# Three edits to the small products of a two-layer trunk: quarters of the array, one stretch of scores, and ends of heads one by one

## The chip, the cores and the metric

The kernel runs on one core of a Trainium2 chip. The metric is the device time in microseconds (us) of one launch, as the median of several runs; lower is better. The core has five engines that each work through their own list of instructions in order: TensorE (PE, matrix products), VectorE (DVE), ScalarE (ACT), GpSimd (POOL) and SyncE (SP), whose queue issues the transfers from memory. Products land in PSUM, in banks of 128 rows by 512 words; everything else lies in SBUF. Both have 128 rows (partitions).

## What is computed

Two layers work on 512 tokens of width 1024, in float32. Layer 0 mixes tokens with two groups of heads over one input projection: four mLSTM heads (64-wide keys, 128-wide values) and four gated DeltaNet heads (128 wide). Layer 1 mixes with eight HGRN2 heads. After each mixer, and after each gated feed-forward part, comes a normalised residual addition.

```python
for layer in range(DEPTH):
    u = rms_norm(x, norm_gains[layer, 0])
    mix = ab_mixer(u, ...) if layer % 2 == 0 else hgrn2_mixer(u, ...)
    x = x + rms_norm(mix, norm_gains[layer, 1])
    u = rms_norm(x, norm_gains[layer, 2])
    x = x + rms_norm(conv_ffn(u, ...), norm_gains[layer, 3])
```

Per chunk of tokens, an mLSTM head does the following; `num / den` is then normalised per head and multiplied by a sigmoid gate:

```python
s = jnp.einsum("bhld,bhsd->bhls", q_, k_) * d
num = jnp.einsum("bhls,bhsv->bhlv", s, v_) + w_inter[..., None] * jnp.einsum("bhld,bhdv->bhlv", q_, C)
den = jnp.sum(s, -1) + w_inter * jnp.einsum("bhld,bhd->bhl", q_, n)
C = carry_decay[..., None, None] * C + jnp.einsum("bhl,bhld,bhlv->bhdv", wk, k_, v_)
```

A DeltaNet head solves a unit lower triangular system per chunk and then scans over the chunks:

```python
sol = lax.linalg.triangular_solve(a_mat, rhs, left_side=True, lower=True, unit_diagonal=True)
v_new = u_ - jnp.einsum("bhld,bhdv->bhlv", w_, state)
o = jnp.einsum("bhld,bhdv->bhlv", qd_, state) + jnp.einsum("bhls,bhsv->bhlv", attn_, v_new)
state = gl_[..., None, None] * state + jnp.einsum("bhld,bhlv->bhdv", kd_, v_new)
```

An HGRN2 head has the same kind of scan, with the state decayed per key dimension. Each head's output is normalised by the root of its mean square and gated.

## The kernel before

The projections run with channels on the partitions and all 512 tokens along the row. Weights arrive by DMA as `raw`; ACT makes a rounded copy `whi` of them, DVE or POOL the remainder `wlo`, and each product of 128x512 is done three times (`whi` with `uh`, `whi` with `ul`, `wlo` with `uh`), 24 of them for one block of 128 channels. In the profile these are `pf` (input projections and feed-forward), `pt` (projections with tokens on the partitions) and `mo` at L127 (output projection). They are called full products here. The heads' own products are small: float32, 128x128 or less. A float32 product leaves two records in the profile, a full product one.

The order of each engine's list is fixed when the kernel is built. A planner walks through the program, puts each instruction where its cost table says it is ready, and fills the wait of a small product with full products of work that is due later. `tc.issue_after(x)` holds back what is issued under it until `x` has its place; `in_a_row` (L1102) uses this to keep a list of products behind its first one. Heads are generators: `run_head` starts one up to its `yield`, and `end_heads` runs the rest of it later, after the next head's projections have been written.

Layer 0 works two heads at a time in the order gdn(0), mlstm(0), gdn(1), mlstm(1).

- `gdn_pair` (L1108) inverts the triangular matrices, 128x128 for each of 4 chunks and 2 heads. Each is built from quarters of 64x64. `doubled` (L1205, with the products at L1210 and L1212) grows the inverse of the diagonal quarters level by level; at last `pp` (L1226) and `pd` (L1230) make the lower left quarter, eight products of 64x64 each: `pp` takes the rows `lo` and puts all eight in the rows `hi`, `pd` goes the other way, with ACT's copy of `pp` between them (L1227). Then each head scans its four chunks (`vn` L1245 and L1247, `S` L1252, `o` L1253 and L1255) and ends: squares on ACT (`chunk_squares`, L754), the root `rsqrt` on DVE (an integer guess and three Newton steps, eleven instructions with the one that makes its argument), then `head_out`: `yn`, four transposes on PE into `yt`, the gate, and the split into `yhi` (ACT) and `ylo` (DVE).
- `mlstm_pair` (L1274) makes 16 score products `ms` (L1298; 64x64 tiles, 128 columns: 4 chunks, 2 heads, 2 halves of the keys), multiplies them by the decays `dec` on DVE, makes 6 state additions `C` (L1305), adds the states up on DVE (`mC`), and then the outputs: 8 products `mo`<-`vaug` (L1320) and 6 `mo`<-`mC` (L1326). The end of both heads follows together: eight squares, one root over 128x8, then `head_out` twice.

Layer 1's mixer `c_mix` works in pairs too; `pair` makes the scores by levels (`lev` from `qf`, `kr`, and at last `mid`), assembles `at`, and for each head transposes the keys (`kdt`), copies them (`kt`), and scans. The last pair is j = 3.

The output projection of each layer needs `yhi` and `ylo` of all eight heads; the products that need the last head come last. Before layer 0's output projection stands mlstm(1), before layer 1's the pair j = 3.

In the token norms, the root uses ACT's Sqrt from a table (`tk_y`), which takes an `ACT_TABLE_LOAD` when another table was in use.

Of the kernel before, what the change touches and what calls it, by code (L numbers as in the profile page):

```python
# [18 lines left out]
P = 128  # L19
S = 512  # L20
D = 1024
NT = S // P
# [12 lines left out]
def kernel(  # L35
# [734 lines left out]
    def gate_block(wcols, u, new, func, eng=None):  # L770

        gs = new("gs")
        A.activation(out=gs, in_=feature_block(wcols, u, eng), func=func)
        return gs


    def ab_mix(pm, u, x0, g0):
# [274 lines left out]
        def decay_t(row, cvec, sub):  # L1052

            ps = mxt("rowbc")
            T.matmul(ps, lhsT=picks[:, row : row + 1].broadcast_to([P, P]), rhs=rows, start=True, stop=True)
            d = s("dec")
            tt(V, v4(d), v4(ps), bc(cvec, P), ALU.subtract if sub else ALU.add)
            G.affine_select(  # L1058
                out=v4(d), in_=v4(d), pattern=[[0, NT], [1, P]], compare_op=ALU.is_ge, fill=-BIG, base=0,
                channel_multiplier=-1,  # L1060
            )
            A.activation(out=d, in_=d, func=AF.Exp)
            return d, ps
# [44 lines left out]
        def gdn_pair(j, k, q, vf, gates):  # L1108
# [108 lines left out]
            for a in range(2):  # L1217
                tt(V, xx[lo, a * NT : (a + 1) * NT], pzs[a][lo, 0], bm(identc[lo], NT), ALU.add)
            for rs in (hi, lo):
                for a in range(2):  # L1220
                    tt(V, v4(mts[a])[rs, :, rs], pzs[a][rs, 1], bm(identc[rs], NT), ALU.add)
            if j == 0:
                fill(32, e)
            pp = chunks(mxt("pp"))
            for c in range(PC):
                T.matmul(pp[hi, c], lhsT=mc[c][lo, hi], rhs=xx[lo, c], start=True, stop=True)  # L1226
            A.copy(out=xx[hi], in_=pp[hi])  # L1227
            pd = chunks(mxt("pd"))
            for c in range(PC):
                T.matmul(pd[lo, c], lhsT=xx[hi, c], rhs=mc[c][hi, hi], start=True, stop=True)  # L1230
            for a in range(2):
                A.copy(out=v4(mts[a])[lo, :, hi], in_=pd[lo, a * NT : (a + 1) * NT])
# [41 lines left out]
        def mlstm_pair(j, k, q, gss):  # L1274
# [9 lines left out]
            ds = [decay_t(2 * j + a, c1[:, :, 2 * j + a], False)[0] for a in range(2)]  # L1284
            pt = mxt("mkt")
# [8 lines left out]
            for c, cs in enumerate(css):  # L1294
                for a, hs in enumerate(heads):
                    for ps in heads:
                        ks = slice(c * P + ps.start, c * P + ps.stop)
                        T.matmul(mss[a][ps, cs], lhsT=k[hs, ks], rhs=q[hs, cs], start=True, stop=True)  # L1298
            for a in range(2):
                tt(V, ds[a], mss[a], ds[a], ALU.mult)  # L1300

            pc = bank("sc", "C")[:, : 3 * (P + 1)].rearrange("p (c n) -> p c n", c=3)
            for c in range(NT - 1):
                for a, hs in enumerate(heads):
                    T.matmul(pc[hs, c], lhsT=v4(kw)[:, c, hs], rhs=vaug[2 * j + a][:, c, :], start=True, stop=True)  # L1305
# [32 lines left out]
            for a in range(2):  # L1338
                chunk_squares(ss[:, 4 * a : 4 * a + 4], hm[:, a])
# [4 lines left out]
            stt(v, ss, 0.5 / P, v, ALU.mult, ALU.add)  # L1344
            r = rsqrt(v, 8, "ml")
            for a in range(2):
                i = 2 * j + a
                ylo[i] = eighth(i, "ylo", F32R)
                head_out(
                    yhi[:, i, :], ylo[i], hm[:, a], r[:, 4 * a : 4 * a + 4], gss[a], bank("sc", "yt"),  # L1350
                    cmix[:, 88 + i : 89 + i],
                )
# [38 lines left out]
    def c_mix(pm, u, first, lb, olb, olbq, cnorm, maskc):  # L1391
# [25 lines left out]
        def pair(j, states, gates):  # L1417
# [104 lines left out]
            gss, pos = gates(), []  # L1522
            for a, (_, _, qk, _) in enumerate(states):
                h = 2 * j + a
                qb, kb, at = qk[:, 0, :], qk[:, 1, :], ats[a]
                for hf in (slice(0, 64), slice(64, P)):
                    A.copy(out=v4(at)[hf, :, hf], in_=atcs[a][hf])
                for i in range(2):
                    A.copy(out=v4(at)[:64, i::2, 64:], in_=pm_[i * 64 : (i + 1) * 64, a])
                tot = tots[a]  # L1530
                pt = bank("sc", "kdt")
                transpose4(pt, kb, range(NT))
                kt = s("kt")
                A.copy(out=kt, in_=pt)
                st = None
# [16 lines left out]
                pos.append(po)  # L1552
            yield
            ss = col(8, "mss")
            for a, po in enumerate(pos):
                chunk_squares(ss[:, 4 * a : 4 * a + 4], v4(po))
            r = mean_rsqrt(ss, 8, P, "ml")
            for a, po in enumerate(pos):
                h = 2 * j + a
                ylo[h] = eighth(h, "ylo", F32R)  # L1560
                head_out(yhi[:, h, :], ylo[h], v4(po), r[:, 4 * a : 4 * a + 4], gss[a], bank("sc", "yt"))
# [32 lines left out]

        def gate(h):
            ps = feature_block(cols_of(3072, h), u, V)
            gs = s("gs")
            A.activation(out=gs, in_=ps, func=AF.Sigmoid)
# [166 lines left out]
```

## Time and profile before

| | |
|---|---|
| median of 3 runs | 1320.03 us (1319.99 to 1321.26) |
| profiled execution | 1320.03 us, span 1318.3 us |
| mean granted TensorE clock | 0.999 |
| PE busy | 1302.2 us, 99% of the span |
| DVE, ACT, POOL busy | 662.6, 603.8, 368.5 us |
| layer 0's mixer | about 10 to 275 us |
| layer 0's feed-forward part | about 275 to 720 us |
| layer 1's mixer | about 720 to 925 us |
| layer 1's feed-forward part | about 925 us to the end |

A row of the timeline reads: start in us, duration in us, engine, line of the kernel, operation, output<-inputs by their names in the program, tile size on PE, shape, xN for N records in one row. Brackets at the end give the idle time of the engine just before, and what ended it. Durations on PE contain the time in its pipeline, so rows overlap; what a product costs PE is read from the start of one row to the start of the next. A row of the windows gives the stretch, its length, then the busy time and number of records of PE, weight loads (PEld), DVE, ACT and POOL, the granted PE clock, the DMA share and GB/s. A row of the waits gives the total in us, how often, and the longest. A row on a tile (`tk_y`) gives the smallest, median and largest duration in ns, and the first and last start.

### The profile page before, as it was taken

The page shows a single profiled execution, that of the slowest core. Times are in us where ns is not written, and L with a number is a line of the kernel's source. Part 1 is how long each engine was busy: PE and PEld are TensorE (multiplying, and loading weights), DVE is VectorE, ACT ScalarE, POOL GpSimd, SP SyncE. Part 2 cuts the span into 40 slices and gives each one's busy share as a digit, 9 for nine tenths or more (in the row PEclk, how much of TensorE's full clock was granted, in tenths as well). Part 3 has the DMA queues.
Part 4 walks back from the last instruction along what each step waited for, and adds up shares of the span by engine and source line. Part 5 has one row for each costly group of instructions (what it writes and reads, how often), then busy time and mean ns, then how long its engine had stood idle before and what let it go on. Part 6 is the DMA issues. An engine that isn't in the chain of part 4 may idle for free.

```text
span 1318.3 us, 19346 instructions
## 1 busy us (share of the span) xinstructions
PE 1302.2 (99%) x7581; PEld 1084.3 (82%) x7581; DVE 662.6 (50%) x1310; ACT 603.8 (46%) x1164; POOL 368.5 (28%) x200
## 2 busy tenths in 40 slices
PE   8999999999999999999999999999999999999998
PEld 8878888879888888888888888887888888888886
DVE  6875684567533333311376784976764333331114
ACT  6764563455433333322456654655554333333222
POOL 1000010002655555544200000000065555554440
PEclk9999999999999999999999999999999999999999
DMA  7521221243333333222305123231243333322211
GB/s 201 144 65 40 63 74 39 81 144 112 113 97 99 99 99 102 94 99 96 112 7 154 65 65 93 83 97 30 84 128 96 96 96 97 99 101 93 98 56 64
DMA packets 164697, 121.18 MB, mean 92 GB/s; under 512 B 8382, under 2 KB 150142, under 8 KB 164606
## 3 DMA queue, kind: packets, MB, share of 16 engines
q1 hardware_dynamic: 164606, 119.94, 29.9%
q8 instruction: 60, 0.98, 0.3%
q14 instruction: 31, 0.25, 0.1%
HBM read 117.83 MB, written 2.10 MB: 91 GB/s over the span
## 4 chain that ended last, share of the span: by engine, by line
PE 90%; ACT 4%; DVE 3%; DMA 1%; issue 1%; POOL 0%; SPq 0%; DVEq 0%; ACTq 0%; POOLq 0%
PE pf L127 49%; PE dn L127 15%; PE mo L124 4%; PE dn L124 3%; PE pf L124 3%; PE pt L127 2%; PE pt L124 2%; PE mo L127 2%; PE lev L1474 1%; PE ut L124 1%; ACT junk L754 1%; DMA raw<-in_ab_w_in_dram 1%; DVE wlo L99 1%; ACT whi L228 1%; DMA raw<-in_c_w_in_dram 1%
## 5 line engine op out<-in xcount | busy, mean ns | idle before, releaser
L99 POOL TENSOR_TENSOR wlo<-raw,whi 128x1024 fp32r<-128x1024 f32 x122 | 294.5, 2415 | 594.7 <-ACT whi L228 587.1
L127 PE MATMUL pf<-ul,whi 128*128 128x512 f32 x1040 | 408.1, 392 | 0.0
L127 PE MATMUL pf<-uh,whi 128*128 128x512 f32 x1040 | 407.2, 392 | 0.0
L127 PE MATMUL pf<-uh,wlo 128*128 128x512 f32 x1040 | 406.5, 391 | 0.0
L228 ACT CAST whi<-raw 128x1024 fp32r<-128x1024 f32 x192 | 201.0, 1051 | 222.0 <-PE pf L127 208.5
L102 DVE SCALAR_TENSOR_TENSOR acc<-pf,fcw,acc 128x511 f32<-128x511 f32 (+1 forms) x176 | 131.8, 749 | 274.2 <-ACT acc L306 271.1
L127 PEld LDWEIGHTS pf<-ul,whi 128*128 128x128 f32 x1040 | 195.3, 188 | 40.0
L127 PEld LDWEIGHTS pf<-uh,whi 128*128 128x128 f32 x1040 | 195.3, 188 | 39.8 <-issue 0.2
L127 PEld LDWEIGHTS pf<-uh,wlo 128*128 128x128 f32 x1040 | 195.3, 188 | 39.5
L99 DVE TENSOR_TENSOR hl<-h,hh 128x512 fp32r<-128x512 f32 x44 | 32.0, 727 | 161.7 <-ACT hh L589 161.7
L127 PE MATMUL dn<-whi,hh 128*128 128x512 f32 x288 | 112.2, 390 | 0.0
L127 PE MATMUL dn<-whi,hl 128*128 128x512 f32 x288 | 112.1, 389 | 0.0
L127 PE MATMUL dn<-wlo,hh 128*128 128x512 f32 x288 | 112.1, 389 | 0.0
L99 DVE TENSOR_TENSOR wlo<-raw,whi 128x1024 fp32r<-128x1024 f32 x70 | 85.1, 1221 | 41.9 <-ACT whi L228 41.5
L589 ACT CAST hh<-h 128x512 fp32r<-128x512 f32 x44 | 27.4, 623 | 155.2 <-PE dn L127 131.5
L1058 POOL TENSOR_SCALAR_AFFINE_SELECT dec<-dec 128x512 f32<-128x512 f32 x8 | 8.4, 1049 | 222.8 <-DVE dec L99 175.6
L306 ACT ACTIVATE acc<-pf,fcb,fcw 128x512 f32<-128x512 f32 x88 | 68.2, 775 | 4.2 <-PE pf L124 3.2
L99 POOL TENSOR_TENSOR sg<-sg,acc 128x512 f32<-128x512 f32 x44 | 57.8, 1313 | 25.5 <-ACT sg L565 25.5
L127 PEld LDWEIGHTS dn<-whi,hh 128*128 128x128 f32 x288 | 54.1, 188 | 11.6 <-issue 0.5
L127 PEld LDWEIGHTS dn<-wlo,hh 128*128 128x128 f32 x288 | 54.1, 188 | 11.3
L127 PEld LDWEIGHTS dn<-whi,hl 128*128 128x128 f32 x288 | 54.1, 188 | 11.2
L565 ACT ACTIVATE sg<-acc 128x512 f32<-128x512 f32 x44 | 27.8, 632 | 68.2 <-DVE acc L102 68.2
(383 smaller groups left out, 1816.3 us busy)
## 6 DMA issues: line engine op xcount, KB each, us to landing
raw<-in_ffn_w_up_dram SPq DMA_DIRECT2D x88, 512.0 KB, 3.7
raw<-in_ffn_w_down_dram SPq DMA_DIRECT2D x44, 512.0 KB, 3.3
raw<-in_c_w_in_dram SPq DMA_DIRECT2D x32, 512.0 KB, 4.3
raw<-in_ab_w_in_dram SPq DMA_DIRECT2D x26, 512.0 KB, 3.6
gain<-in_norm_gains_dram SPq DMA_DIRECT2D x8, 512.0 KB, 3.7
raw<-in_ab_w_out_dram SPq DMA_DIRECT2D x8, 512.0 KB, 3.7
raw<-in_c_w_out_dram SPq DMA_DIRECT2D x8, 512.0 KB
x<-in_x_dram SPq DMA_DIRECT2D x4, 512.0 KB
```

The source lines that it names most:

```text
L99: return eng.tensor_tensor(out=o, in0=a, in1=b, op=op)
L102: return V.scalar_tensor_tensor(out=o, in0=a, scalar=s, in1=b, op0=op0, op1=op1, **kw)
L124: last[eng] = f(**kw)
L127: f(**kw)
L228: A.copy(out=hv, in_=rv)
L306: A.activation(out=acc, in_=ps, func=AF.Identity, scale=taps[:, K - 1 : K], bias=bias)
L565: A.activation(out=sg, in_=ag, func=AF.Sigmoid)
L589: A.copy(out=hi, in_=hT[k])
L754: A.activation(out=junk[:, :P], in_=src[:, c, :], func=AF.Square, accum_out=ss[:, c : c + 1])
L1058: G.affine_select(out=v4(d), in_=v4(d), pattern=[[0, NT], [1, P]], compare_op=ALU.is_ge, fill=-BIG, base=0, channel_multiplier=-1,)
L1474: e = T.matmul(pls[a][i * 64 : (i + 1) * 64, c], lhsT=krs[a][:, c * P + i * 64 : c * P + (i + 1) * 64], rhs=qfs[a][:, :, at : at + 32], st ...
```

## The change

1. The inverse's last products. `pp` alternates between head 1 and head 0, and head 1's results go to the rows `lo` instead of `hi`; the second head's factors get a tile `x1` of their own (tag `sig`, one more DVE addition). `pd` alternates too, into two PSUM banks, with rows `lo` for head 1 and `hi` for head 0. ACT copies `pp` in two halves. Both sequences are kept by `in_a_row`.
2. The mLSTM's scores and additions. One `in_a_row` holds the addition of chunk 0 and head 1, then all 16 scores (by chunk, then half of the keys, then head), then the other five additions. Before, the scores' order was chunk, head, half. The two multiplications by the decays follow the stretch.
3. The last two heads of a layer. mLSTM pair 1 and the pair j = 3 of layer 1 end one head after the other: four squares, a root over 128x4 and `head_out` for the first, then for the second. The root is `table_rsqrt`: Sqrt on ACT, then a reciprocal, two multiplications and one combined step on DVE. `load_roots` does a Sqrt of ones ahead of it, behind the last gate and, in layer 0, the last decay. For j = 3, both heads' key transposes and copies come first (the second copy in tag `f`), then both scans, then the ends.

```diff
+    def table_rsqrt(v, n, st):
+        y, q = col(n, st + "_y"), col(n, st + "_q")
+        A.activation(out=y, in_=v, func=AF.Sqrt, scale=2.0)
+        V.reciprocal(out=y, in_=y)
+        tt(V, q, y, y, ALU.mult)
+        tt(V, q, q, v, ALU.mult)
+        r = col(n, st + "_y")
+        stt(r, q, 1.5, y, ALU.subtract, ALU.mult, reverse0=True)
+        return r
+
+    def load_roots(*after):
+        one = col(1, "tk_y")
+        V.memset(one, 1.0)
+        with ExitStack() as st:
+            for e in after:
+                st.enter_context(tc.issue_after(e.ins))
+            A.activation(out=one, in_=one, func=AF.Sqrt)
...
+            x1 = chunks(s("sig"))
+            tt(V, x1[lo, :NT], pzs[1][hi, 1], bm(identc[hi], NT), ALU.add)
+            pp = chunks(mxt("pp"))
+
+            def first(c, a):
+                ac = a * NT + c
+                return T.matmul(pp[(hi, lo)[a], ac], lhsT=mc[ac][lo, hi], rhs=xx[lo, ac], start=True, stop=True)
+
+            in_a_row(first, [(c, a) for c in range(NT) for a in (1, 0)])
...
-            pp = chunks(mxt("pp"))
-            for c in range(PC):
-                T.matmul(pp[hi, c], lhsT=mc[c][lo, hi], rhs=xx[lo, c], start=True, stop=True)
-            A.copy(out=xx[hi], in_=pp[hi])
-            pd = chunks(mxt("pd"))
-            for c in range(PC):
-                T.matmul(pd[lo, c], lhsT=xx[hi, c], rhs=mc[c][hi, hi], start=True, stop=True)
+            A.copy(out=xx[hi, :NT], in_=pp[hi, :NT])
+            A.copy(out=x1[lo, NT:], in_=pp[lo, NT:])
+            pds = [chunks(mxt("pd")) for _ in range(2)]
+
+            def second(c, a):
+                lhs, rhs = (x1[lo, NT + c], x1[lo, c]) if a else (xx[hi, c], mc[c][hi, hi])
+                return T.matmul(pds[a][lo, c], lhsT=lhs, rhs=rhs, start=True, stop=True)
+
+            in_a_row(second, [(c, a) for c in range(NT) for a in (1, 0)])
...
+            if j:
+
+                load_roots(last["gate"], last["decay"])
...
-            for c, cs in enumerate(css):
-                for a, hs in enumerate(heads):
-                    for ps in heads:
-                        ks = slice(c * P + ps.start, c * P + ps.stop)
-                        T.matmul(mss[a][ps, cs], lhsT=k[hs, ks], rhs=q[hs, cs], start=True, stop=True)
...
+            in_a_row(
+                either,
+                [(added, 0, 1)]
+                + [(score, c, part, a) for c in range(NT) for part in range(2) for a in range(2)]
+                + [(added, c, a) for c in range(NT - 1) for a in range(2) if c or not a],
+            )
...
-            r = rsqrt(v, 8, "ml")
...
+            for heads in ((0,), (1,)) if j else ((0, 1),):
+                cs = slice(NT * heads[0], NT * (heads[-1] + 1))
+                n = NT * len(heads)
+                for a in heads:
+                    chunk_squares(ss[:, 4 * a : 4 * a + 4], hm[:, a])
+                stt(v[:, cs], ss[:, cs], 0.5 / P, v[:, cs], ALU.mult, ALU.add)
+                r = table_rsqrt(v[:, cs], n, "hn") if j else rsqrt(v, n, "ml")
...
+            if j == 3:
+
+                load_roots(gated[A])
...
+                kts.append(s("f" if a and j == 3 else "kt"))
+                A.copy(out=kts[a], in_=pt)
+                if j == 3:
+                    continue
+                scan(a)
+            if j == 3:
+
+                scan(0)
+                scan(1)
+                ends(j, pos, gss, (0,), table_rsqrt)
+                yield
+                ends(j, pos, gss, (1,), table_rsqrt)
+                return
             yield
...
+            ends(j, pos, gss, (0, 1), rsqrt)
```

The order in which the engines get the instructions changes with it. On PE, in layer 0's pair 0, the scores stood among the products of the delta rule's scan (`S`, `o`, `vn`) before:

```order
L1298 MATMUL ms<-q,k 64x128
L1252 MATMUL S<-vn,kd 128x128
L1253 MATMUL o<-vn,dec 128x128
L1255 MATMUL o<-gS,qd 128x128
L1245 MATMUL vn<-v,mt 128x128
L1298 MATMUL ms<-q,k 64x128 x4
L1247 MATMUL vn<-gS,wt 128x128
L1298 MATMUL ms<-q,k 64x128 x3
L127 MATMUL pf<-uh,whi 128x512
```

In the changed kernel the same pair has, behind the `yt` of the delta rule's second head:

```order
L258 MATMUL yt<-ident,yn 128x128 x4
L1339 MATMUL C<-vaug,kd 64x129
L1333 MATMUL ms<-q,k 64x128 x16
L1339 MATMUL C<-vaug,kd 64x129 x5
L127 MATMUL pf<-uh,wlo 128x512
L1368 MATMUL mo<-vaug,dec 128x129 x8
L1374 MATMUL mo<-mC,qd 128x129 x6
```

All scores have moved behind the scan and that `yt`, and the additions stand around them. Between the scan's last `o` and the `yt` there are 29 full products now. In pair 1, 17 full products stand between the last `mo`<-`mC` and the first `yt`, where 27 stood, and eight between the two `yt`, where seven stood.

On DVE, the chain from the squares of that second head (`hss`) to its `yn` ran without anything between before. Now its last part reads:

```order
L99 TENSOR_TENSOR hn_q<-hn_y 128x4
L99 TENSOR_TENSOR wlo<-raw,whi 128x1024
L99 TENSOR_TENSOR hn_q<-hn_q,hn_v 128x4
L102 SCALAR_TENSOR_TENSOR k<-pf,cmix,k 128x511
L102 SCALAR_TENSOR_TENSOR hn_y<-hn_q,hn_y 128x4
L102 SCALAR_TENSOR_TENSOR k<-pf,cmix,k 128x510
L99 TENSOR_TENSOR yn<-o,hn_y 128x512
L102 SCALAR_TENSOR_TENSOR k<-pf,cmix,k 128x509
```

A remainder of weights and the convolution steps of the next pair's `k` have come in among the root's steps; before, the convolution stood behind `yn`.

On ACT, at the end of layer 1's mixer, the list before was:

```order
L1534 COPY kt<-kdt 128x512
L754 ACTIVATE junk,mss<-o 128x128 x6
L767 CAST yhi<-y 128x512 x2
```

and it is now:

```order
L1609 COPY f<-kdt 128x512
L774 ACTIVATE junk,hss<-o 128x128 x4
L206 ACTIVATE hn_y<-hn_v 128x4
L774 ACTIVATE junk,hss<-o 128x128 x4
L206 ACTIVATE hn_y<-hn_v 128x4
L787 CAST yhi<-y 128x512 x2
```

The squares of the two heads have a root (`hn_y`, Sqrt) behind each four. On PE, six full products stand between the last `o` there and the first `yt` (19 before), and ten between the two `yt`, where one stood.

More of the change, by code (lines that the diff above doesn't have):

```diff
@@ L772, in gate_block @@
         gs = new("gs")
-        A.activation(out=gs, in_=feature_block(wcols, u, eng), func=func)
+        last["gate"] = A.activation(out=gs, in_=feature_block(wcols, u, eng), func=func)
         return gs
@@ L1061, in decay_t @@
             )
-            A.activation(out=d, in_=d, func=AF.Exp)
+            last["decay"] = A.activation(out=d, in_=d, func=AF.Exp)
             return d, ps
@@ L1293, in mlstm_pair, with score, added, either @@
             mss = [mxt("ms") for _ in range(2)]
-            for c, cs in enumerate(css):
-                for a, hs in enumerate(heads):
-                    for ps in heads:
-                        ks = slice(c * P + ps.start, c * P + ps.stop)
-                        T.matmul(mss[a][ps, cs], lhsT=k[hs, ks], rhs=q[hs, cs], start=True, stop=True)
+            def score(c, part, a):
+                ps = heads[part]
+                ks = slice(c * P + ps.start, c * P + ps.stop)
+                return T.matmul(mss[a][ps, css[c]], lhsT=k[heads[a], ks], rhs=q[heads[a], css[c]], start=True, stop=True)
+            pc = bank("sc", "C")[:, : 3 * (P + 1)].rearrange("p (c n) -> p c n", c=3)
+            def added(c, a):
+                return T.matmul(
+                    pc[heads[a], c], lhsT=v4(kw)[:, c, heads[a]], rhs=vaug[2 * j + a][:, c, :], start=True, stop=True
+                )
+            def either(f, *what):
+                return f(*what)
+            in_a_row(
[3 more added lines that the diff above has]
+                + [(added, c, a) for c in range(NT - 1) for a in range(2) if c or not a],
+            )
             for a in range(2):
                 tt(V, ds[a], mss[a], ds[a], ALU.mult)
[L1302 to L1305, printed above, removed]
             Cs = []
@@ L1343, in mlstm_pair @@
             stt(v.rearrange("p (a c) -> p a c", a=2), den, 0.5 * EPS, den, ALU.mult, ALU.mult)
-            stt(v, ss, 0.5 / P, v, ALU.mult, ALU.add)
-            r = rsqrt(v, 8, "ml")
[L1346 to L1352, printed above, removed]
+            for heads in ((0,), (1,)) if j else ((0, 1),):
[5 more added lines that the diff above has]
+                r = table_rsqrt(v[:, cs], n, "hn") if j else rsqrt(v, n, "ml")
+                for a in heads:
+                    i = 2 * j + a
+                    ylo[i] = eighth(i, "ylo", F32R)
+                    head_out(
+                        yhi[:, i, :], ylo[i], hm[:, a], r[:, NT * (a - heads[0]) :][:, :NT], gss[a], bank("sc", "yt"),
+                        cmix[:, 88 + i : 89 + i],
+                    )
         def gdn(j):
@@ L1521, in pair, with scan @@
                         )
[L1522 to L1535, printed above, removed]
+            gss, pos, kts = gates(), [], []
+            if j == 3:
+                load_roots(gated[A])
+            def scan(a):
+                h, at, kt, tot = 2 * j + a, ats[a], kts[a], tots[a]
+                qb, st = states[a][2][:, 0, :], None
                 po = bank("po" if a else "mx", "o")
@@ L1593, in front @@
             return k, q, qk, f
+        gated = {}
         def gate(h):
@@ L1597, in gate @@
             gs = s("gs")
-            A.activation(out=gs, in_=ps, func=AF.Sigmoid)
+            gated[A] = A.activation(out=gs, in_=ps, func=AF.Sigmoid)
             stt(gs, ps, cnorm[:, h : h + 1], gs, ALU.mult, ALU.mult)
```

28 lines of the change are left out of this document (19 added, 9 removed).

## The prediction

> **What bounds the kernel now.** I read the busy times first, then the chain that ended last, then the windows by stage, and last the timeline of TensorE at the places that the change touches.
>
> ```profile
> PE 1302.2 (99%) x7581; PEld 1084.3 (82%) x7581; DVE 662.6 (50%) x1310; ACT 603.8 (46%) x1164; POOL 368.5 (28%) x200
> PE 90%; ACT 4%; DVE 3%; DMA 1%; issue 1%; POOL 0%; SPq 0%; DVEq 0%; ACTq 0%; POOLq 0%
> 105.00:145.00 40.00, 40.00 (x280) 32.11 (x279) 22.62 (x66) 20.36 (x50) 2.58 (x2) 1.00 0.15 43
> PE S L1541 <- ACT kt L1534: 0.3, 1, 0.3
> ```
>
> TensorE (PE) is busy 99% of the span and holds 90% of the chain; in the window from 105 to 145 us, where layer 0's small products stand, it is busy 40.00 of 40.00 us at a granted clock of 1.00, with DMA at 0.15. Wherever a small product waits for ScalarE (ACT) or VectorE (DVE), projection products of 128x512 are put ahead of it, so a microsecond that PE needs less is a microsecond of the end, as long as no stall takes it back. So I count PE time at each place, then the stalls.
>
> **The last products of the inverse, `pp` and `pd`.**
>
> ```profile
> 105.93 1.14 PE L1226 MATMUL pp<-PR,mt 64*64 64x64 f32 x16
> 107.00 0.50 PE L127 MATMUL pf<-uh,whi 128*128 128x512 f32 x1
> 108.12 1.14 PE L1230 MATMUL pd<-mt,PR 64*64 64x64 f32 x16
> 87.20 1.15 PE L1180 MATMUL pz<-identc,mt 64*64 64x64 f32 x32
> 88.28 0.50 PE L127 MATMUL pf<-uh,whi 128*128 128x512 f32 x1
> 100.02 0.70 PE L1210 MATMUL pz<-PR,xt 64*64 64x64 f32 x32
> 100.54 0.66 PE L1212 MATMUL pz<-xt,PR 64*64 64x64 f32 x32
> 101.12 0.50 PE L127 MATMUL pf<-ul,whi 128*128 128x512 f32 x1
> ```
>
> A matmul leaves two records. The 16 records of `pp`, all in one 64x64 quarter, hold PE from 105.93 to 107.00: 1.07 us. `pz` at 87.20, spread over quarters, puts 32 records in 1.08 us, and the two groups from 100.02, over all four, put 64 in 1.10 us. So a quarter does a record in some 0.058 us and another quarter works beside it. Two quarters save 8 of the 16 turns, 8 x 0.058 = 0.47 us; with `pp` and `pd` in both pairs of heads that is 4 x 0.47 = **1.87 us**. ACT's one copy between `pp` and `pd` becomes two and DVE gets one more addition; four projection products, 0.93 us, cover the copies, which is about what two short copies take. If the new pairs of quarters don't overlap the term is 0.
>
> **The scores and state additions of the mLSTM.** Pair 1 first, where they stand nearly together already, then pair 0:
>
> ```profile
> 254.13 0.40 PE L127 MATMUL mo<-wlo,yhi 128*128 128x512 f32 x1
> 254.46 1.09 PE L1298 MATMUL ms<-q,k 64*64 64x128 f32 x16
> ...
> 256.61 0.43 PE L1305 MATMUL C<-vaug,kd 128*64 128x129 f32 x2
> 256.97 0.50 PE L127 MATMUL mo<-whi,yhi 128*128 128x512 f32 x1
> ...
> 257.63 1.09 PE L1298 MATMUL ms<-q,k 64*64 64x128 f32 x16
> 258.65 0.88 PE L1305 MATMUL C<-vaug,kd 128*64 128x129 f32 x10
> 259.46 2.05 PE L1320 MATMUL mo<-vaug,dec 128*128 128x129 f32 x16
> ```
> ```profile
> 128.90 0.40 PE L127 MATMUL pf<-uh,wlo 128*128 128x512 f32 x1
> 129.23 0.43 PE L1298 MATMUL ms<-q,k 64*64 64x128 f32 x2
> ...
> 132.60 0.40 PE L127 MATMUL pf<-ul,whi 128*128 128x512 f32 x1
> ...
> 133.50 0.39 PE L1245 MATMUL vn<-v,mt 128*128 128x128 f32 x2
> ...
> 135.50 0.39 PE L1255 MATMUL o<-gS,qd 128*128 128x128 f32 x2
> ...
> 136.64 0.48 PE L127 MATMUL pf<-uh,wlo 128*128 128x512 f32 x1
> ...
> 140.45 0.66 PE L238 MATMUL yt<-ident,yn 128*128 128x128 f32 x4
> 141.04 0.89 PE L1305 MATMUL C<-vaug,kd 128*64 128x129 f32 x12
> 141.85 1.61 PE L1320 MATMUL mo<-vaug,dec 128*128 128x129 f32 x12
> ```
>
> A full product starts some 0.23 us after the one before it. From 254.13 to 259.46 are 5.33 us, with seven full products in them (1.62): scores and additions cost 3.71, and about 0.1 more for the way back to 128x128 tiles ahead of `mo`. What a change of tile shape costs shows at 257.63: 16 score records take 1.02 us to the next group's start, while eight turns of two, at no more than 2 x 0.058 for 128 columns instead of 64, make 0.93. In pair 0, from 128.90 to 132.60 (3.70 us) the other work is two full products and five of 128x128 (0.223 each): 1.58. From 133.50 to 136.64 (3.14) it is five small ones: 1.12. The scores' six pieces thus cost 2.12 + 2.02 = 4.14 us, far over the 1.86 of their 16 turns: the rest is the change of tile shape there and back, nearly 0.4 us a piece. The additions add 0.81 and about 0.2 of changes: 5.15.
>
> Afterwards there is one stretch: about 0.10 to enter, 0.36 for the first addition (256.61 to 256.97), the scores, 0.81 for the other five additions, 0.11 to leave. The scores' order by chunk, part, head puts four neighbouring products on four quarters; before, the pairs ran two and two. I take four at a time, as `pz` does, so 32 records take what 16 took, 1.02 us. Sum 2.40; saved 3.81 - 2.40 = 1.41 in pair 1, and 5.15 - 2.40 = 2.75 in pair 0, together **4.16 us**. Bounds: if the scores stay two and two, the stretch is 0.9 longer in each pair, and 2.4 remains; above, at most 0.2 more, if `C` and the scores follow each other without a change.
>
> **The ends of the last two heads.**
>
> ```profile
> 262.99 0.31 ACT L754 ACTIVATE junk<-hm 128x128 bf16<-128x128 f32 x1
> 266.47 0.17 DVE L102 SCALAR_TENSOR_TENSOR ml_v<-mss,ml_v 128x8 f32<-128x8 f32 x1 [2.99 <-ACT junk L754]
> 269.53 0.63 PE L238 MATMUL yt<-ident,yn 128*128 128x128 f32 x4 [0.76 <-DVE yn L99]
> 910.87 0.17 DVE L205 TENSOR_SCALAR ml_v<-mss 128x8 f32<-128x8 f32 x1 [2.24 <-ACT junk L754]
> 913.09 0.69 DVE L99 TENSOR_TENSOR yn<-o,ml_y 128x512 f32<-128x512 f32 x1
> 913.83 0.66 PE L238 MATMUL yt<-ident,yn 128*128 128x128 f32 x4 [0.34 <-DVE yn L99]
> 915.92 0.50 PE L127 MATMUL mo<-whi,yhi 128*128 128x512 f32 x1 [1.43 <-ACT yhi L767]
> L124 ACT ACTIVATE tk_y<-tr_v x32: 192/203/206, 6.1 to 1312.9; 128x1 f32<-128x1 f32 x32
> ```
>
> In layer 0, eight squares take 262.99 to 266.47, 0.435 each; in layer 1 the eleven steps of the root, its argument among them, take 910.87 to 913.09, 2.2 us at 0.2 each. Done one head after the other, four squares (1.7 us) stand ahead of the first root instead of eight, and the root is six steps, Sqrt among them at 0.20, with two hand-overs between engines: some 1.4 us. The first `yt` is ready about 1.7 + 0.8 = 2.5 us earlier. But its cover shrinks: in layer 0 the order leaves 17 full products ahead of it where 27 stood, 10 x 0.23 = 2.3 us less; of the 0.9 or so that PE loses there now (0.76 idle, and a change of shape) 0.2 to 0.3 is won, and a part of that goes again at the second `yt`, which has eight products of cover, 1.9 us: a gain of only **0.15** (between -0.6 and +0.7, the root being estimated). In layer 1 before, 0.3 (`S` for `kt`), 0.4 at 913.83 and 1.5 at 915.92 are lost, 2.2 us with the changes of shape. Afterwards the second transpose stands ahead of the scans (`S` no longer waits), the second scan and six full products lie ahead of the first `yt` (some 4.0 us against a chain of some 4.2), and ten products lie between the two `yt`, where one stood: the 1.5 us have their cover. I keep 0.45 as lost: **+1.75**, bounds 0.3 and 2.2.
>
> **What the change costs.** Bringing Sqrt forward puts a table load on ACT:
>
> ```profile
> 252.77 1.28 ACT L1062 ACT_TABLE_LOAD   x1
> 254.07 0.63 ACT L1062 ACTIVATE dec<-dec 128x512 f32<-128x512 f32 x1
> ```
>
> 1.28 us, and the next activation follows at once. In layer 1 it stands behind the last gate, just ahead of the copies `qf` and `mid`, which `lev` needs: I give it **0.1 us** on PE, bounds 0 and 1.3. In layer 0 it stands behind the last decay, and the load ahead of the output stage's first root goes.
>
> "ScalarE: Activation LUTs" of the Trainium skill, under What ACT_TABLE_LOAD costs, puts about 1.38 us of drain on top of each load. The rows show none; by that rule `lev` would start 1.4 us later.
>
> A new stall stands in pair 0, at the `yt` of the delta rule's second head:
>
> ```profile
> 128.86 1.22 DVE L99 TENSOR_TENSOR wlo<-raw,whi 128x1024 fp32r<-128x1024 f32 x1
> 145.82 0.75 DVE L102 SCALAR_TENSOR_TENSOR k<-pf,cmix,k 128x511 f32<-128x511 f32 x1 [0.36 <-ACT k L304]
> ```
>
> DVE's order now puts one `wlo` and two of the next head's convolution steps between the steps of its root: 1.13 + 0.66 + 0.66 = 2.45 us on a chain that took 4.95 from its last `o` (135.50) to its `yt` (140.45). Between these two products there are now 29 full ones, 6.65 us, with the `o` itself and its change of shape 6.9 to 7.0, against 7.4: I charge **0.5**, between 0 (they fill gaps of the root's steps) and 1.3 (a convolution step waits for its projection too). Behind this `yt` the whole stretch of scores is queued, and behind that the pair's outputs. Also, the two multiplications of the scores by the decay now come one after the other, and the second head's `mo` may wait for it: 2 x **0.05**.
>
> Sum: 1.87 + 4.16 + 0.15 + 1.75 - 0.1 - 0.5 - 0.1 = **7.2 us**. The profiled execution took 1320.03 us, with a span of 1318.3; this is also the median of the three runs. **1320.0 - 7.2 = 1312.8 us.**
>
> **The rivals.**
> A. *The quarters don't share the array further.* Scores stay two and two: 1.8 less, 1314.6; `pp` and `pd` too: 1316.5. For it: no row has 128-column products on four quarters. Against it: the 64 records in 1.10 us.
> B. *The table load hits PE.* Should `mid` come 1.4 us later, `lev` stops PE by about 1.3, and the whole kernel takes 1314.1. Against it: 252.77 and 254.07 leave no room. This is what the page's drain would make.
> C. *New stalls take the place of the old.* The `yt` at 1.3 instead of 0.5, the first addition waiting for `kd`, layer 0's end at -0.6, layer 1's at 0.3: up to 3.5 us back, 1316.3. For it: DVE's order in pair 0. Against it: six to 29 full products stand ahead of each.
> D. *No change.* Most of A, B and C together: 1317.5 to 1320. The change would then not do what it says, since a single stretch pays its shape changes once whatever the quarters do.
> E. *Slower.* Denser small products lower TensorE's granted clock. Place: from the mixers on; price: 1% of 1302 us is 13.0 us, 1325.8; it decides from 0.55%, where it eats the 7.2. Against it: the clock is 1.00 in the window where PE is busy 40.00 of 40.00 us.
>
> **How the numbers follow.** My forecast 0.62 (1311 to 1314.5), A 0.10, B 0.08, C 0.11, D 0.05, E 0.04. This kernel's measurement tells about 0.2%, 2.6 us, from no change: faster is below 1317.4. The forecast, A, B and C lie there: 0.91 with a small part of C beyond it, so faster 0.90, same 0.06, slower 0.04. The range 1309.8 to 1316.8 takes in A, B and C, and 3 us below for terms I may have put too low, the price of a change of shape above all.
>
> **What would show it.** Right: `pp` and `pd` in some 0.6 us each; one stretch of 32 score records in about 1.0 us between additions; PE without the 1.43 us wait for `yhi` in layer 1, and the small one of about 0.5 us at `yt` near 138 us. Wrong: scores at 1.9 us, a wait of `lev` for `mid` over 0.5 us, a `yt` wait in layer 0 over 1.3 us, or PEclk below 1.00.

## The result, and the profile after

The changed kernel takes 1312.17 us (median of four), the kernel before 1320.45 us in the same comparison. The ratio is 0.9936, with a 95% interval of 0.9916 to 0.9955: 8.3 us less, where 7.2 were forecast (1312.8 us). Four more runs of it on another chip (e12) gave 1312.24 us. One of the first four executions of the change took 2163.78 us at a granted clock of 0.556, and one of e1's ten 2246.17 us at 0.644; the ratios leave these two out, and what slowed them was not found.

The page of the changed kernel, its span, busy times and granted clock, and the waits of PE (total us, times, longest us):

```profile
span 1310.2 us, 19354 instructions
PE 1295.1 (99%) x7581; PEld 1079.7 (82%) x7581; DVE 662.4 (51%) x1312; ACT 607.2 (46%) x1173; POOL 368.5 (28%) x200
PEclk9999999999999999999999999999999999999999
PE ut L124 <- DVE un L124: 2.1, 1, 2.1
...
PE lev L1526 <- DVE qf L99: 0.6, 1, 0.6
PE pz L1230 <- ACT PR L1212: 0.6, 1, 0.6
PE yt L258 <- DVE ml_v L102: 0.4, 1, 0.4
...
PE S L1587 <- ACT kt L1609: 0.3, 1, 0.3
...
PE yt L258 <- DVE yn L99: 0.2, 1, 0.2
```

PE is busy 7.1 us less, with the same 7581 records, and the span is 8.1 us shorter. Of the 7.1 us, 0.9 are no gain: at the start the products `warm`, which come ahead of the first data, hold PE for 4.77 instead of 5.67 us, and PE then waits 2.1 instead of 1.1 us at the first `ut`, which starts at 7.97 us where it started at 7.86. The wait of `mo` for `yhi`, 1.4 us before, is gone from the list. The clock is where it was.

Where the time went is read from places that both traces have, in the same order:

| place | before, us | after, us | earlier by |
|---|---|---|---|
| first output product `mo` at L124, layer 0 | 277.16 | 270.59 | 6.57 |
| first `dn`, layer 0 | 548.29 | 541.72 | 6.57 |
| first `lev`, layer 1 | 721.10 | 714.82 | 6.28 |
| first `mo` at L124, layer 1 | 920.73 | 912.57 | 8.16 |
| last product | 1311.44 | 1303.29 | 8.15 |

The feed-forward parts contribute nothing, layer 0's mixer 6.57 us, layer 1's mixer 1.88, and 0.29 is lost ahead of the first `lev`.

The timeline of PE in the changed kernel, first `pp` and `pd`, then pair 0's stretch, then the end of layer 0 and of layer 1:

```profile
106.18 0.68 PE L1246 MATMUL pp<-PR,mt 64*64 64x64 f32 x16
106.79 0.50 PE L127 MATMUL pf<-uh,wlo 128*128 128x512 f32 x1
...
107.92 0.27 PE L1260 MATMUL pd<-sig 64*64 64x64 f32 x1
...
108.53 0.50 PE L127 MATMUL pf<-uh,whi 128*128 128x512 f32 x1
...
132.83 0.39 PE L1287 MATMUL o<-gS,qd 128*128 128x128 f32 x2
...
139.43 0.39 PE L127 MATMUL pf<-ul,whi 128*128 128x512 f32 x1
139.94 0.66 PE L258 MATMUL yt<-ident,yn 128*128 128x128 f32 x4
140.53 0.43 PE L1339 MATMUL C<-vaug,kd 128*64 128x129 f32 x2
140.89 1.10 PE L1333 MATMUL ms<-q,k 64*64 64x128 f32 x32
141.92 0.88 PE L1339 MATMUL C<-vaug,kd 128*64 128x129 f32 x10
142.73 0.50 PE L127 MATMUL pf<-uh,wlo 128*128 128x512 f32 x1
143.07 1.95 PE L1368 MATMUL mo<-vaug,dec 128*128 128x129 f32 x16
...
261.23 0.39 PE L127 MATMUL mo<-whi,yhi 128*128 128x512 f32 x1
262.06 0.63 PE L258 MATMUL yt<-ident,yn 128*128 128x128 f32 x4 [0.44 <-DVE ml_v L102]
...
891.74 0.45 PE L1553 MATMUL lev<-mid 128*64 128x64 f32 x8
...
903.09 0.40 PE L127 MATMUL mo<-wlo,yhi 128*128 128x512 f32 x1
903.56 0.66 PE L258 MATMUL yt<-ident,yn 128*128 128x128 f32 x4
...
906.50 0.60 PE L258 MATMUL yt<-ident,yn 128*128 128x128 f32 x4
```

`pp` holds PE for 0.61 us instead of 1.07, and so does `pd`. The 32 score records take 1.03 us, what 16 took in pair 1 before. The first `yt` of layer 0's end waits 0.44 instead of 0.76 us, and in layer 1 the two `yt` come almost without a wait. `lev` does not wait for `mid` (891.74 carries no bracket), though the table load stands ahead of ACT's copies `mid` (887.33 to 888.61).

### The profile page after: what moved, and what is told of

It reads as the page before. It is cut to its first block, busy times and chain, and to the rows that moved or that the text cites. A ratio compares the mean times of both kernels' runs of the same rounds, so it can differ in the third digit from the quotient of the medians.

```text
span 1310.2 us, 19354 instructions
## 1 busy us (share of the span) xinstructions
PE 1295.1 (99%) x7581; PEld 1079.7 (82%) x7581; DVE 662.4 (51%) x1312; ACT 607.2 (46%) x1173; POOL 368.5 (28%) x200
## 4 chain that ended last, share of the span: by engine, by line
PE 90%; ACT 3%; DVE 3%; DMA 1%; issue 1%; POOL 0%; SPq 0%; DVEq 0%; ACTq 0%; POOLq 0%
PE pf L127 49%; PE dn L127 15%; PE mo L124 4%; PE dn L124 3%; PE pf L124 3%; PE pt L127 3%; PE mo L127 2%; PE pt L124 2%; PE lev L1526 1%; PE ut L124 1%; DVE wlo L99 1%; ACT junk L774 1%; DMA raw<-in_c_w_in_dram 1%; ACT whi L248 1%; PE pz L1230 1%
```

## The experiments

The changed kernel is called "the change" here. Ratios are against the kernel before on the same chip, with 95% intervals. There were three chips, on which the kernel before took 1320.58 us (e1 to e4), 1320.38 us (e5 to e8) and 1320.81 us (e9 to e12). The change itself stands beside e9, e10 and e11 as e12; other differences to it are between chips and carry a few tenths more doubt.

| run | what | median us | ratio |
|---|---|---|---|
| e1 | only the quarters of `pp`, `pd` | 1318.76 | 0.9985 (0.9975 to 0.9995) |
| e2 | only the stretch of scores | 1318.95 | 0.9991 (0.9982 to 1.0) |
| e11 | e2 once more | 1320.45 | 0.9995 (0.9986 to 1.0005) |
| e3 | only the ends one by one | 1317.85 | 0.9978 (0.9969 to 0.9988) |
| e4 | the change, scores in the old written order | 1312.83 | 0.9943 (0.9928 to 0.9958) |
| e9 | the change, scores head by head | 1313.59 | 0.9946 (0.9931 to 0.9961) |
| e7 | the change, scores ahead of all additions | 1315.69 | 0.9963 (0.9948 to 0.9978) |
| e8 | the change, additions between the chunks | 1314.67 | 0.9955 (0.994 to 0.997) |
| e10 | the change, additions ahead of the scores | 1312.21 | 0.9937 (0.9922 to 0.9952) |
| e5 | the change, table not brought forward | 1312.13 | 0.9934 (0.9918 to 0.9951) |
| e6 | the change, the old root | 1313.35 | 0.9944 (0.9929 to 0.9959) |
| e12 | the change again | 1312.24 | 0.9938 (0.9923 to 0.9953) |

### Each edit alone

e1 takes only the part of the diff in `gdn_pair`, e2 only the scores and additions of `mlstm_pair`, e3 all the rest.

> The kernel before with only the first edit: pp and pd alternate between two quarters. Theory (a quarter works beside another): pp and pd take about 0.61 us each instead of 1.07, 0.46 saved four times, 1.87 us in all: 1318.2 us. Rival (these quarters do not share the array, or the two copies between pp and pd make PE wait): pp and pd stay at 1.07, or a wait of about 0.4 us before pd: 1320.0 us.

Measured: 1318.76 us. In the profile of e1 `pp` starts at 106.51 and the product behind it at 107.12:

```profile
106.51 0.68 PE L1226 MATMUL pp<-PR,mt 64*64 64x64 f32 x16
107.12 0.50 PE L127 MATMUL pf<-uh,wlo 128*128 128x512 f32 x1
```

0.61 us, as the theory says, and 0.61 for `pd` too (108.25 to 108.86). The rival falls. The median is 1.8 us under that of before (1320.58), where 1.87 was expected.

> The kernel before with only the third edit: ends of the last two heads one by one, root from the Sqrt table. Theory (cover for the first yt and for the yhi of layer 1's last head): 0.3 us in layer 0 and 1.75 us in layer 1: 1318.0 us. Rival (the table load ahead of the copies mid delays lev, by 1.3 us): 1319.3 us, with a wait of PE at lev for mid.

Measured: 1317.85 us, 2.7 less than before by the medians and 2.15 by the profiled executions. `lev` waits for no `mid`. By the places of the table above, layer 0's end is 0.23 us earlier at its first `mo` of L124, and from the first `lev` to layer 1's first `mo` of L124 e3 takes 197.75 us where before took 199.63: 1.88 less. The theory holds.

> The kernel before with only the second edit: scores and additions in one stretch, scores over four quarters. Theory (four quarters, and every change of tile shape costs some 0.35 us there and back): 4.16 us saved, less about 0.1 us at the yt of pair 0's delta rule and up to 0.6 us at the second yt at the end of layer 0, which the order here gives four full products of cover instead of seven: 1316.0 to 1316.6 us; scores 1.03 us in each pair. Rival one (changes of shape are free, only the quarters count): 2 x 0.9 saved, 1318.2 us. Rival two (the scores stay two and two): scores 1.9 us, about 1318 us.

Measured: 1318.95 us, from 1316.44 to 1322.25, a scatter that neither theory nor rivals foresaw; the median lies above all their times. The profiled execution was the fastest, and it is as the theory says: one stretch with 32 score records in 1.03 us, a time of 1316.44 us, the first `mo` of L124 3.71 us earlier than before, and a new wait of 0.6 us at the second `yt` at the end of layer 0. So the kernel was run again.

> The kernel before with only the second edit, once more: its times lay 2 to 6 us above the one that was profiled. Theory (the scatter belongs to those executions, not to the kernel): most runs at 1316.4 to 1317 us. Rival (this kernel is really slower than its profiled execution): 1318.6 us and more again.

Measured: 1320.45 us, from 1318.62 to 1322.12, so the theory of a single odd occasion falls, and the rival stands: every run but the profiled one of e2 lies 2.2 to 5.8 us above that. By the medians the second edit alone gains 1.6 and 0.4 us, and both intervals reach 1. The second profile has a span of 1319.3 against 1314.7 us, and shows where that time lies. The waits of PE in e11:

```profile
PE lev L1487 <- DVE qf L99: 1.9, 1, 1.9
...
PE mcol L1039 <- DVE dec L1027: 0.5, 1, 0.5
PE pz L1212 <- issue: 0.5, 1, 0.5
PE pt L127 <- issue: 0.3, 1, 0.3
```

None of these is at the scores, whose 32 records take 1.04 us in e11. The first output product of layer 0 is 1.73 us later than in e2's profile, the first `lev` another 1.37 (VectorE's `qf` comes later), and layer 1's mixer takes 1.47 more. That last part lies right behind the wait of `mo` for `yhi`, which before, e1 and e2 have too. Rows of PE in e11, and a row of the windows:

```profile
915.43 0.50 PE L127 MATMUL mo<-whi,yhi 128*128 128x512 f32 x1 [1.43 <-ACT yhi L767]
...
917.40 0.63 PE L127 MATMUL mo<-whi,yhi 128*128 128x512 f32 x1
917.83 0.63 PE L127 MATMUL mo<-wlo,yhi 128*128 128x512 f32 x1
```
```profile
915.00:919.00 4.00, 3.57 (x11) 3.01 (x12) 2.54 (x5) 1.86 (x4) 0.00 (x0) 0.60 0.00 0
```

From 915 to 919 us the granted clock is 0.60, and full products start 0.43 us apart instead of 0.23. In e2's profile the same wait stands at 912.33, and the products behind it keep to 0.23. The times of whole executions agree. Of the 45 executions of the kernel before beside these experiments, the 14 with a mean granted clock of 0.997 took 1320.8 to 1322.2 us, the other 31 took 1319.5 to 1321.3. In e11 the five at 0.997 took 1320.3 to 1322.1 us, the other five 1318.6 to 1321.3. Kernels with the third edit, which removes this wait, show 0.997 in none of the 45 executions that the ratios use. So in some executions the wait seems to cost about 1.4 us beyond its own length. That it brings the drop on is suggested by this and not shown, since only one execution with the drop has a profile.

The rest of the scatter, above all the 1.9 us at the first `lev`, is open. The times of e2 and e11 therefore tell little of the second edit; what it is worth beside the other two is read from e7, below.

### What makes the scores fast

e4 changes one line inside the stretch:

```diff
-                + [(score, c, part, a) for c in range(NT) for part in range(2) for a in range(2)]
+                + [(score, c, part, a) for c in range(NT) for a in range(2) for part in range(2)]
```

> The changed kernel, but inside the stretch the scores come in the old order (chunk, head, half of the keys), all else as changed. Theory (four neighbouring products on four quarters run side by side, two neighbours on two quarters only two and two): the scores take about 1.9 us instead of 1.03, 0.87 more in each pair: 1313.9 us. Rival (the order does not matter, the stretch alone makes the gain): 1312.2 us.

Measured: 1312.83 us, between the two, and in the profile of e4 the scores take 1.03 us, as in the change. It has waits of 0.46 and 0.39 us at `pz` near 198 and 202 us, which the change's profile has not.

```profile
141.02 1.10 PE L1333 MATMUL ms<-q,k 64*64 64x128 f32 x32
142.05 0.88 PE L1339 MATMUL C<-vaug,kd 128*64 128x129 f32 x10
```

The theory falls, and with it a sentence of the prediction: the order in which the program writes the scores is not what kept them from the four quarters. The instruction list of before shows what did. There the planner put all eight scores of head 0 (their PSUM tile is `ms_1666`) ahead of those of head 1 (`ms_1667`). The number in front is the row's place in PE's list, in which equal neighbours make one row:

```
580 L1298 MATMUL ms_1666<-q_1521,k_1484 64x128
585 L1298 MATMUL ms_1666<-q_1521,k_1484 64x128 x4
587 L1298 MATMUL ms_1666<-q_1521,k_1484 64x128 x3
594 L1298 MATMUL ms_1667<-q_1521,k_1484 64x128
596 L1298 MATMUL ms_1667<-q_1521,k_1484 64x128 x4
599 L1298 MATMUL ms_1667<-q_1521,k_1484 64x128 x3
```

A head's scores read one half of the rows, so only two quarters were in use at a time. `in_a_row` keeps the written order, and the two written orders that alternate the heads within four products, the change's and e4's, both use all four. e9 writes the order that the planner had chosen:

```diff
-                + [(score, c, part, a) for c in range(NT) for part in range(2) for a in range(2)]
+                + [(score, c, part, a) for a in range(2) for c in range(NT) for part in range(2)]
```

> The changed kernel, with the scores of one head all ahead of those of the other inside the stretch: two quarters at a time, as the planner of the kernel before had them, and nothing else of the stretch changed. Theory (the gain of the scores is half quarters, half changes of shape): scores 1.9 us instead of 1.03 in each pair, 1313.9 us. Rival (two quarters are as fast as four, only the changes of shape count): scores 1.03 us, 1312.2 us.

Measured: 1313.59 us, 1.35 more than the change beside it (e12). The profile of e9:

```profile
140.99 1.59 PE L1333 MATMUL ms<-q,k 64*64 64x128 f32 x32
142.51 0.88 PE L1339 MATMUL C<-vaug,kd 128*64 128x129 f32 x10
```

1.52 us: the rival falls, since two quarters are slower than four, but 1.9 was too much. The start times of the single records tell why. Within a head two records start together every 0.109 us; around the middle five pairs follow each other at 0.05 to 0.06 us. There the first scores of head 1 already run beside the last of head 0, on the other half of the rows, which saves the 0.38 us; the two records at 141.49 have the 0.32 us that the first two of head 0 have. In the change four records start together every 0.109 us. The two stretches of e9 are each 0.49 us longer than the change's (pair 1's scores go from 252.93 to 254.45). That is 0.98 of the 1.35 us; the rest is not found at the scores.

e7 puts the scores ahead of all six additions:

```diff
-                [(added, 0, 1)]
-                + [(score, c, part, a) for c in range(NT) for part in range(2) for a in range(2)]
-                + [(added, c, a) for c in range(NT - 1) for a in range(2) if c or not a],
+                [(score, c, part, a) for c in range(NT) for part in range(2) for a in range(2)]
+                + [(added, c, a) for c in range(NT - 1) for a in range(2)],
```

> The changed kernel with the scores ahead of all six additions in the list; the planner then pulls the scores of pair 0 back into the delta rule's scan in six pieces and those of pair 1 into two, but they keep the order over four quarters. Theory (each piece pays its change of shape, some 0.35 us): pair 0 costs about 2.0 us more and pair 1 about 0.5, less 0.1 at the yt: 1314.6 us. Rival (the quarters make the gain, pieces cost nothing): 1312.2 us or a little less.

Measured: 1315.69 us, more than the theory gave. The profile of e7 in pair 0 has the six pieces of before, to the hundredth:

```profile
128.21 0.43 PE L1333 MATMUL ms<-q,k 64*64 64x128 f32 x2
...
129.66 0.65 PE L1333 MATMUL ms<-q,k 64*64 64x128 f32 x8
...
130.66 0.65 PE L1333 MATMUL ms<-q,k 64*64 64x128 f32 x6
131.24 0.50 PE L127 MATMUL pf<-uh,whi 128*128 128x512 f32 x1
```

The planner had put the scores head by head again, in both pairs, so this run has neither the stretch nor the four quarters: what it was to test, pieces that keep the four quarters, did not come about. It is the change without its second edit, and so the measure of that edit in its place: 1315.69 - 1312.24 = 3.45 us, or 3.56 against e5 on the same chip. The forecast has 4.16 saved at the scores, less what is lost at the `yt`.

e8 spreads the additions among the scores:

```diff
-                + [(score, c, part, a) for c in range(NT) for part in range(2) for a in range(2)]
-                + [(added, c, a) for c in range(NT - 1) for a in range(2) if c or not a],
+                + [(score, 0, part, a) for part in range(2) for a in range(2)]
+                + [(added, 0, 0)]
+                + [(score, 1, part, a) for part in range(2) for a in range(2)]
+                + [(added, 1, 0)]
...
+                + [(score, 3, part, a) for part in range(2) for a in range(2)]
+                + [(added, 2, 0), (added, 2, 1)],
```

> The changed kernel with an addition put between the scores of one chunk and the next: the same products in the same stretch, with six more changes between 64x64 and 128x64 tiles in each pair. Theory (a change of shape costs 0.1 to 0.17 us): 0.6 to 1.0 us more in each pair, 1313.4 to 1314.2 us. Rival (only the way from and to 128x128 costs): 1312.2 us.

Measured: 1314.67 us, 2.4 more than the change. The profile of e8, the stretch of pair 0:

```profile
140.94 0.43 PE L1339 MATMUL C<-vaug,kd 128*64 128x129 f32 x2
141.31 0.45 PE L1333 MATMUL ms<-q,k 64*64 64x128 f32 x8
141.69 0.43 PE L1339 MATMUL C<-vaug,kd 128*64 128x129 f32 x2
...
143.92 0.44 PE L1339 MATMUL C<-vaug,kd 128*64 128x129 f32 x4
144.29 0.50 PE L127 MATMUL pf<-uh,wlo 128*128 128x512 f32 x1
```

From 140.94 to 144.29 are 3.35 us, against 2.20 in the change (140.53 to 142.73), for the same products with six more changes between the two tile shapes: 1.15 us more, at most 0.19 a change. A part is not the change of shape. The additions of the two heads go to different halves of the columns, and as neighbours they run side by side: in e10, below, the six make three turns of two (140.70, 140.98 and 141.20 us, the last taking some 0.22). Here four of the six stand alone, which makes five turns, against some four in the change. With 0.22 taken off, an estimate, some 0.15 us a change remain. Twice 1.15 is 2.3 of the 2.4 us measured. The rival, that only the way from and to 128x128 costs, falls.

e10 uses that price:

```diff
-                [(added, 0, 1)]
-                + [(score, c, part, a) for c in range(NT) for part in range(2) for a in range(2)]
-                + [(added, c, a) for c in range(NT - 1) for a in range(2) if c or not a],
+                [(added, c, 1 - a) for c in range(NT - 1) for a in range(2)]
+                + [(score, c, part, a) for c in range(NT) for part in range(2) for a in range(2)],
```

> The changed kernel with all six additions ahead of the 16 scores: one change between 64x64 and 128x64 tiles less in each pair, and four full products instead of one between the stretch and mo. Theory (a change costs 0.18 us, as the run with more changes showed): 0.36 us less, 1311.8 us, and a stretch of 2.0 instead of 2.2 us in the profile. Rival (the outputs now wait for the decay products, which start later behind the scores): no gain, 1312.2 to 1312.8 us, with a wait of PE at mo for dec.

Measured: 1312.21 us, against 1312.24 for the change beside it. Neither side is right. The profile of e10, pair 1, and a wait that it has:

```profile
252.90 0.89 PE L1339 MATMUL C<-vaug,kd 128*64 128x129 f32 x12
253.71 1.10 PE L1333 MATMUL ms<-q,k 64*64 64x128 f32 x32
254.75 0.50 PE L127 MATMUL mo<-wlo,yhi 128*128 128x512 f32 x1
```
```profile
PE pz L1230 <- ACT PR L1212: 1.2, 2, 0.6
```

The stretch takes 1.85 us, 0.35 less than in the change in each pair and twice what the expectation gave: one change of shape less, at about 0.15, and one turn less, since no addition stands alone. `mo` does not wait. But `pz` waits for ACT's `PR` a second time, 0.60 us at 197.77, which the profile of the change does not have. In this execution that takes back most of the 0.70 us of both pairs. The same place varies in other runs (0.46 us there in e4, 0.41 in e5), so whether the wait belongs to this version is open. By its times it is no better than the change.

> The changed kernel itself, beside the three others on the same chip: 1312.2 us.

Measured: 1312.24 us.

### The ends

e5 takes both calls of `load_roots` out of the change.

```diff
-            if j:
-                load_roots(last["gate"], last["decay"])
...
-            if j == 3:
-                load_roots(gated[A])
```

> The changed kernel without bringing the Sqrt table forward: the table load of 1.28 us now stands between the first head's squares and its Sqrt in both layers. The order moves six full products ahead of the first yt in layer 0 and about eight in layer 1. Theory (a load costs its 1.28 us and nothing behind it, and the products moved ahead cover it): 1312.2 to 1312.9 us. Rival (a drain of about 1.4 us stands behind the load): the first yt of both layers waits 1.4 us longer, about 1315 us.

Measured: 1312.13 us, as the change. The profile of e5 on ACT, at layer 1's end, from the last square of the first head to the first square of the second:

```profile
902.08 0.19 ACT L774 ACTIVATION_READ_ACCUMULATOR junk<-o 128x1 f32 x1
902.29 1.28 ACT L206 ACT_TABLE_LOAD   x1
903.59 0.20 ACT L206 ACTIVATE hn_y<-hn_v 128x4 f32<-128x4 f32 x1
903.70 0.26 ACT L774 ACTIVATE junk<-o 128x128 bf16<-128x128 f32 x1
```

The load takes 1.28 us, and the Sqrt starts 0.02 us after it: no drain shows. And the load need not come early. With the load inside the chain, the planner put more full products ahead of the first `yt` (23 instead of 17 in layer 0), and the output projection had them to spare.

e6 does the same and uses the old root:

```diff
-                r = table_rsqrt(v[:, cs], n, "hn") if j else rsqrt(v, n, "ml")
+                r = rsqrt(v[:, cs], n, "hn") if j else rsqrt(v, n, "ml")
...
-                ends(j, pos, gss, (0,), table_rsqrt)
-                ends(j, pos, gss, (1,), table_rsqrt)
+                ends(j, pos, gss, (0,), rsqrt)
+                ends(j, pos, gss, (1,), rsqrt)
```

> The changed kernel with the old root on VectorE (eleven steps) in place of the table, the heads still one by one. The first yt is ready about 0.8 us later in both layers; the order moves three full products (0.7 us) ahead of it in layer 0 and some in layer 1, and fewer are left behind the second yt. Theory (the gain comes from ending the heads one by one, the root adds little): 1312.4 to 1313.2 us. Rival (the short root makes the gain): the 1.9 us of layer 1 are lost, 1314 us or more.

Measured: 1313.35 us (1312.38 to 1313.98), the profiled execution being the fastest. In its profile layer 1's mixer, from the first `lev` to the first `mo` of L124, takes 198.12 us, against 197.64 in e12 and 199.63 before. So three quarters of layer 1's gain come without the short root; the root itself adds some 0.5 us there, and layer 0's end costs nothing (271.04 us at the first `mo` of L124, against 271.07). The rival, that the root makes the gain, falls. The median is 1.1 us above e12's, a little beyond the theory's range; the other 0.6 us are in no profile.

## Why the prediction was right

**What bounds the kernel.** PE stayed at 99% with the same records. The places in the table moved by what PE saved at the edits and by the waits that went. The step holds.

**`pp` and `pd`.** 0.61 us for `pp` and, from 107.92 to 108.53, for `pd`; 1.87 us were forecast for all four, and e1 measured 1.8 by the medians. In pair 1 of the change they take 0.62 (208.13 to 208.75) and 0.61.

**Scores and additions.** From 140.53 pair 0's stretch shows the forecast pieces: 0.36 for the first addition, 1.03 for the scores, 0.81 for the others, 0.11 to leave. The sum of 2.40 us a pair was right. The reason for the four quarters was not. The prediction laid it to the order in which the scores are written; e4 and e9 show that the planner's order by head was the cause, and that the unbroken stretch mended it. How the gain divides is less sure. e9 gives 1.35 us by the medians, 0.98 in its profile, for four quarters instead of two; e7 gives 3.45 for the whole edit. So some 2.1 to 2.5 us are left for joining the pieces. That is a difference between runs on different chips, and the heads of e9 overlap by 0.38 us at the seam, so four quarters against two are worth somewhat more than e9 shows. And as a time of its own the edit did not show the 4.16 us: alone it gained 1.6 and 0.4.

**The end of layer 0.** Forecast 0.15 us, measured 0.3 (0.76 to 0.44 us of idle time); 0.23 in e3. Within the bounds.

**The end of layer 1.** Forecast 1.75 us less 0.1 for the table load, measured 1.88, in the change and in e3 alike, with no loss at `mid`. One row was misread on the way: the wait of `S` for `kt`, 0.3 us, was put at the last pair. It stands at 739 us, in the first, and it is still there after the change (0.3 us in the list above). At the last pair that wait was 0.1 us. The sum came out because the wait of 1.43 us carries it and the cover was judged a little too low.

**The new stall at `yt` in pair 0.** Forecast 0.5 us, measured 0.12: from the last `o` at 132.83 to the `yt` at 139.94 are 7.1 us, not 7.4. The chain grew by 2.16 us and not by 2.45, since VectorE did `wlo` and the convolution steps partly in the time in which the root's steps wait for each other (they take 0.16 us and start 0.20 apart): here the bound of 0 was nearer than the value taken. The second head's `mo` does not wait (no such row), where 0.1 had been charged.

**The sum.** Forecast 7.2, profile 8.1. The stalls charged too high make 0.5 of the difference, the ends 0.4. Places that no edit touches make the rest: before, PE stood 0.4 us at a `pt` near 201 us, put down to "issue", which the profile of the change does not show; and the first `lev` of layer 1 waits 0.3 us more. The first `ut` also starts 0.1 us later. This is one execution against one, and other profiles show that these places vary, so they belong to no term.

**The rivals.** A (no further sharing) is refuted by the 1.03 and 0.61 us. B (the table load hits `lev`) is refuted by 891.74 and by e5. "ScalarE: Activation LUTs" of the Trainium skill, under What ACT_TABLE_LOAD costs, adds a drain of about 1.38 us to each load; the trace of e5 shows 0.02 us between load and Sqrt. C (new stalls take the place) came true in small: 0.12 us at the `yt`. The 0.44 us in layer 0 are what is left of an old stall. D (no change) is out: the interval ends at 0.9955. E (denser small products lower the clock) did not happen: 0.999 in both profiles. What e11 shows points the other way, a lower clock behind a wait, which this change removes.

## What to carry to other kernels

Count small products by turns and by changes of tile shape, each read from start to start in the timeline: here a piece of two score records cost 0.36 us (e7, 128.21 to 128.57) and one of eight over four quarters 0.38 (e8, 141.31 to 141.69), and joining pieces won at least as much as using more of the array. Products that can share the array must stand next to each other in the instruction list, so look at the list that the planner makes and not at the order in the program. A late table load cost nothing here (e5), and a longer chain about 0.5 us (e6), because the queue of the busiest engine had other work to put ahead of the waiting product.

## What the runs showed that was not expected

The price of changing between 64x64 and 128x64 tiles without a 128x128 product between: 0.15 to 0.19 us (e8).

Products of one half of the rows overlap with those of the other half only near the seam: in e9 by three to four turns (0.38 us of 0.109 each), then each head runs alone. What limits this reach was not tested.

A granted clock of 0.60 between 915 and 919 us, right behind a wait of PE of only 1.43 us (e11), in an execution in which PE is busy 98% of the span.

A stretch of layer 0 near 198 to 204 us that no edit touches varies from profile to profile. PE waits there between 0 and 1.0 us in all, for `PR` of ACT or with nothing but "issue" named: e1 0.55 and 0.39, e2 none, e11 0.35 and 0.46. The start of layer 1 varies too, from 0.1 (e9) to 1.9 us (e11) at the first `lev`. What sets them was not found. Differences under about 1 us between two profiles should not be read as gains unless they are found at the edited place.
